# Splitting the branch weights and branch B's result once, ahead of the products that use them

## The chip, the cores and the metric

The kernel runs on one core of a Trainium2 chip. The metric is the device time of one execution in microseconds (us), the median over runs. Five engines work beside each other, each through its own instructions in order: PE (TensorE, matmuls; its weight loads are listed as PEld), DVE (VectorE), ACT (ScalarE), POOL (GpSimd) and SP (SyncE, which here only issues DMA transfers).

## The reference

One layer over 2048 latent tokens and 256 context tokens, width 1024. What matters here:

```
p = layernorm_modulated(x) @ w_in + b_in          # q,k,v, z_A, decays, x_in, B, C, z_B, g_a, g_b
o_a = gated delta rule, 8 heads, both directions, chunks of 64, over q, k, v
y_a = rmsnorm(o_a) * o_norm_w * silu(z_a)
y_b = B * (conv3(C * x_in) + bias) * silu(z_B)
merged = sigmoid(g_a) * (y_a @ w_a) + sigmoid(g_b) * (y_b @ w_b)
out = layernorm(alpha * x + gate * (merged @ w_out)) * ln_g + ln_b
```

All is float32. `w_a` and `w_b` are 1024 x 1024.

## The kernel before

Large products are made in two parts. A float32 operand is split into a high part (a cast to `float32r`) and a low part (the operand less its high part), and a product is three matmuls: high x high, high x low, low x high. `split` (L350) is that: one cast on ACT (L352) and one subtraction (L353) on POOL, or on DVE where the caller asks.

The program has three stages.

1. **Projections** (`projections`, `units`, `strassen`). Tokens are taken in two pairs of 512. Each pair has 40 units (4 each of k, v and q, 16 of branch B, 12 of gates), and a unit is a block of 256 columns of `w_in`, multiplied by a 2x2 Strassen-like scheme of seven products of 12 matmuls. After each product `run_due` (L831) counts one tick and runs what `later` (L827) has put down for that tick. The results go to DRAM tensors: q, k, v, gates, and branch B's `y_b` (`yb_d`), which `evac_z` (L568) writes as plain float32, 256 KB for each 128 x 512 tile.
2. **Window** (`window`). The delta rule walks 36 chunk visits (18 chunks in two directions). The order on PE is written out by hand; the other engines' orders come from a planner. Each visit is a long chain of small DVE steps: decays (L140), the 16 x 16 inverse by 15 rounds of shuffle, multiply and add (L191 to L193), Gram products (L167), state updates (L302, L333). Between the visit's own matmuls PE takes about 24 matmuls of the branch products out of the generator `fillers`. There are eight jobs in it, four of `y_b @ w_b` and then four of `y_a @ w_a`; a job is a block of 512 tokens, with eight products `m` of 24 matmuls. A job's operand is eight tiles `ah`/`al`, filled by `feed` (L1162); a product's weights come from `load_w` (L337).
3. **Tail** (`final`). What is left of the jobs runs while the operands of `w_out` are prepared (`self.tail` is true, and the splits of weights use DVE), then the output projection and the layer norm.

In the window and the tail, `load_w` loads a 512 KB block of raw weights (128 partitions, eight pieces of 512 B each) and splits it: 64 times in all, since each of the two matrices is loaded by four jobs. `feed` loads `y_b` or `y_a` and splits it, 32 times for each:

```
raw = self.wp.tile([P, KT, n], F32, name="wraw", bufs=2)
nc.sync.dma_start(raw, src[:, c0:c0 + n].rearrange("(k p) n -> p k n", p=P))
return self.split_w(raw, n)
```

The load for product `m + 1` is written behind the third group of matmuls of product `m`.

Of the kernel before, what the change touches and what calls it, by code (L numbers as in the profile page):

```python
# [7 lines left out]
F32 = mybir.dt.float32  # L8
FR = mybir.dt.float32r
# [6 lines left out]
P = 128  # L16
D = 1024
KT = 8
H = 8
# [18 lines left out]
class Kern:  # L38
# [297 lines left out]

    def load_w(self, src, c0, n=P):  # L337

        nc = self.nc
        raw = self.wp.tile([P, KT, n], F32, name="wraw", bufs=2)  # L340
        nc.sync.dma_start(raw, src[:, c0:c0 + n].rearrange("(k p) n -> p k n", p=P))
        return self.split_w(raw, n)

    def split_w(self, raw, n=P):
        wh = self.wp.tile([P, KT, n], FR, name="wh")
        wl = self.wp.tile([P, KT, n], FR, name="wl")
        self.split(wh, wl, raw, self.tail and self.nc.vector)
        return wh, wl

# [15 lines left out]
    def build(self, I, out):  # L365
# [15 lines left out]
        self.v_d = [dt(f"vd{i}", [n // P, P, H, P]) for i, n in enumerate(lens)]  # L381
        self.yb_d = [dt(f"ybd{i}", [H, P, 512]) for i in range(4)]
        self.za_d = [dt(f"zad{i}", [4, P, H, P]) for i in range(4)]
# [47 lines left out]
    def projections(self, es, eb, cp):  # L431
# [15 lines left out]
        for c in ORDER:  # L447
            bp = br if c in LATE else bl
            for k in range(4):
                self.B[c, k] = bp.tile([P, 512], FR, name=f"bh{c}{k}"), bp.tile([P, 512], FR, name=f"bl{c}{k}")  # L450
        self.eh = ExitStack()
        self.hc = self.pool(self.eh, "hc", side="right").tile([P, KT, 256], F32, name="hc")
# [34 lines left out]
        with self.tc.manual_schedule(engines={mybir.EngineType.PE}):  # L487
            for _ in steps:
                pass

    def tokens_of(self, t):
# [5 lines left out]
    def units(self, pair):  # L497
# [26 lines left out]
        for kind, base in (("k", 8), ("v", 16), ("q", 0)):  # L524
            for h in range(0, H, 2):
                def evac(i, j, src, kind=kind, ct=base + h, h=h):
                    self.qkv_out(src, ct + i, kind, h + i, tts(j), 512)
                add((base + h) * P, evac)
                if pair == 0 and kind == "v":
                    out[-1]["ctx"] = lambda i, ps, h=h: self.qkv_out(ps, 16 + h + i, "v", h + i, 4, 256)  # L530
            if kind == "v" and pair == 0:
                out[-1]["after"] = self.eh.close
            if kind == "k":
                out[-1]["after"] = lambda: self.later(4, root)
# [4 lines left out]
        def branch(m):  # L539
# [28 lines left out]
            def evac_z(i, j, src):  # L568
                zs = c11() if (i, j) == (0, 0) else src
                nc.scalar.activation(out=zs, in_=src, func=AF.Silu, bias=col(3, i))  # L570
                nc.vector.tensor_tensor(out=zs, in0=zs, in1=t[i, j], op=ALU.mult)
                nc.sync.dma_start(self.yb_d[tts(j)][m + i], zs)

# [97 lines left out]
    def renew(self):  # L671

        nc = self.nc
        tiles = {}

        def load(c):
            for k in range(4):
                tiles[c, k] = self.bt.tile([P, 512], F32, name="bt")
                nc.sync.dma_start(tiles[c, k], self.t_d[k]["1732564".index(c)])

        for c in ORDER[:2]:
            load(c)
        for i, c in enumerate(ORDER):
            for k in range(4):
                self.split(*self.B[c, k], tiles.pop((c, k)), nc.vector if k % 2 else None)
            if i + 2 < 7:
                load(ORDER[i + 2])
            yield

    def gate_rows(self, pool):  # L690
# [462 lines left out]
    def window(self, es, settle):  # L1153
        tc, nc, I = self.tc, self.nc, self.I
        fa = es.enter_context(tc.tile_pool(name="fa", bufs=1, side="right", reuse_waits="tile"))
        fe = es.enter_context(tc.tile_pool(name="fe", bufs=2, side="right", reuse_waits="tile"))
        w_b, w_a = I["w_b"][0], I["w_a"][0]

        self.gk = self.pool(self.ek, "gk", side="right")
        cur = {k: (fa.tile([P, 512], FR, name=f"ah{k}"), fa.tile([P, 512], FR, name=f"al{k}")) for k in range(KT)}  # L1160

        def feed(src, k, eng=None):  # L1162
            if self.yx and k in (3, 4):
                yr = self.yx.tile([P, 512], F32, name=f"yx{k}")
            else:
                yr = fe.tile([P, 512], F32, name="yr", bufs=3)
            nc.sync.dma_start(yr, src[k])
            self.split(*cur[k], yr, eng)
# [23 lines left out]
        ready = lambda j: j[0] == "b" or done.issuperset(GROUPS[j[1]])  # L1192
        operand = lambda j: (self.yb_d if j[0] == "b" else self.ya_d)[j[1]]

        self.job_at, self.tail = 0, False

        for k in range(KT):
            feed(operand(jobs[0]), k, nc.vector if k % 2 else None)
        w0 = self.load_w(w_b, 0)
        while self.pending:  # L1200
# [4 lines left out]
        def fillers():  # L1205
# [3 lines left out]
            for jn, job in enumerate(jobs):  # L1209
# [6 lines left out]
                if not fed:  # L1216
                    for k in range(KT):
                        feed(operand(job), k, nc.vector if self.tail and k % 2 else None)
                W = w_b if job[0] == "b" else w_a
                w = w or self.load_w(W, 0)  # L1220
# [3 lines left out]
                for m in range(8):  # L1224
# [4 lines left out]
                    for k in range(KT):  # L1229
# [6 lines left out]
                        if m == 7 and fed:  # L1236
                            feed(operand(nxt), k, nc.vector if self.tail and k % 2 else None)
                        if k == 2 and m < 7:
                            w = self.load_w(W, (m + 1) * P)
                        if k < KT - 1:  # L1240
# [387 lines left out]
```

## Time and profile before

| | |
|---|---|
| median of 3 runs | 3256.98 us (3252.83 to 3262.17) |
| the profiled execution's own time | 3256.67 us |
| its span (first to last instruction) | 3255.0 us |
| busy share of the span: PE, DVE, POOL, ACT | 91%, 71%, 50%, 48% |
| moved by DMA | 481.75 MB, mean 148 GB/s |
| mean granted TensorE clock | 0.958 |

A busy share is a mean over stages with different limits, so the stages are read one by one: the projections end at about 1818 us of the span, the window at about 2930 us, the last branch product at about 3064 us. A busy PE is not PE at its peak, since matmuls overlap. A line of the code can be that of a helper: L352 and L353 are all splits, told apart by their tiles.

### The profile page before, as it was taken

How to read it: one execution, taken by the hardware profiler on the slowest of the kernel's cores; microseconds unless marked ns; L12 is line 12 of the kernel's file. 1: busy time of each engine (PE TensorE's matmuls, PEld its weight loads, DVE VectorE, ACT ScalarE, POOL GpSimd, SP SyncE). 2: the span in 40 equal slices, each digit the busy share in tenths (PEclk: the TensorE clock that was granted, in tenths of full speed). 3: DMA queues.
4: the chain of work that ended last, by engine and by line, in shares of the span. 5: the costliest groups of instructions: out<-in, count | busy, mean ns of one | idle time of the engine just before them, and what ended most of it. 6: DMA issues, size and time to landing. Idle time of an engine off the chain costs nothing.

```text
span 3255.0 us, 60533 instructions
## 1 busy us (share of the span) xinstructions
PE 2961.8 (91%) x22089; PEld 2438.2 (75%) x22089; DVE 2296.2 (71%) x5815; ACT 1562.2 (48%) x3453; POOL 1622.9 (50%) x1156
## 2 busy tenths in 40 slices
PE   7899999999998899999999888888888888898987
PEld 4677778888886777888888677777777677786766
DVE  7656645555655664555732679999998999978699
ACT  4664633333456645333344355555555666664221
POOL 3444557766666554666666343343343234425464
PEclk9999999999999999999999989989989889999999
DMA  5533322224564432222233655565566667667742
GB/s 211 143 103 89 101 69 88 85 72 148 179 180 141 113 96 78 71 72 65 85 118 91 211 175 177 170 198 173 173 204 217 207 225 239 226 215 247 229 139 101
DMA packets 423047, 481.75 MB, mean 148 GB/s; under 512 B 25428, under 2 KB 324949, under 8 KB 421724
## 3 DMA queue, kind: packets, MB, share of 16 engines
q1 hardware_dynamic: 413646, 470.43, 46.1%
q10 hardware_dynamic: 9102, 7.45, 0.7%
q8 instruction: 173, 2.83, 0.4%
q14 instruction: 126, 1.03, 0.1%
HBM read 341.32 MB, written 136.47 MB: 147 GB/s over the span
## 4 chain that ended last, share of the span: by engine, by line
PE 46%; DVE 29%; issue 7%; ACT 5%; DMA 5%; POOL 4%; SPq 0%; DVEq 0%; POOLq 0%; ACTq 0%
PE pd L747 12%; PE pd L748 12%; PE pd L749 12%; DVE rb L192 4%; DVE gcb L140 4%; DVE R L193 3%; POOL al L353 2%; DVE rb L191 2%; DMA gcb<-gcd 2%; POOL s L733 1%; DVE t L992 1%; ACT n L177 1%; DVE N L167 1%; PE pst L320 1%; DVE QK L167 1%
## 5 line engine op out<-in xcount | busy, mean ns | idle before, releaser
L747 PE MATMUL pd<-bh,ah 128*128 128x512 f32 x2240 | 888.8, 397 | 10.0 <-ACT u L767 5.8
L749 PE MATMUL pd<-bh,al 128*128 128x512 f32 x2240 | 876.1, 391 | 0.0
L748 PE MATMUL pd<-bl,ah 128*128 128x512 f32 x2240 | 875.5, 391 | 0.0
L353 POOL TENSOR_TENSOR al<-s,ah 128x512 fp32r<-128x512 f32 x348 | 478.7, 1378 | 413.7 <-ACT ah L352 397.3
L353 POOL TENSOR_TENSOR al<-raw,ah 128x512 fp32r<-128x512 f32 x260 | 365.2, 1407 | 338.9 <-ACT ah L352 305.8
L747 PEld LDWEIGHTS pd<-bh,ah 128*128 128x128 f32 x2240 | 423.2, 189 | 97.8 <-issue 6.6
L749 PEld LDWEIGHTS pd<-bh,al 128*128 128x128 f32 x2240 | 422.6, 189 | 90.3 <-POOL al L353 0.2
L748 PEld LDWEIGHTS pd<-bl,ah 128*128 128x128 f32 x2240 | 423.4, 189 | 84.8
L352 ACT CAST ah<-s 128x512 fp32r<-128x512 f32 x352 | 215.5, 619 | 332.9 <-PE pd L748 305.8
L352 ACT CAST ah<-raw 128x512 fp32r<-128x512 f32 x264 | 162.6, 617 | 242.4 <-PE pd L748 205.9
L733 DVE TENSOR_TENSOR s<-s,raw 128x512 f32<-128x512 f32 x80 | 119.7, 1497 | 221.1 <-POOL s L733 221.1
L1235 PE MATMUL pf<-ah,wl 128*128 128x512 f32 x512 | 221.5, 433 | 5.3 <-DVE wl L353 3.1
L1231 PE MATMUL pf<-ah,wh 128*128 128x512 f32 x512 | 214.8, 420 | 11.2 <-DVE R L193 5.4
L1233 PE MATMUL pf<-al,wh 128*128 128x512 f32 x512 | 215.3, 421 | 7.5 <-POOL al L353 3.7
L192 DVE TENSOR_TENSOR rb<-rb,n 128x8 f32<-128x8 f32 (+6 forms) x540 | 202.7, 377 | 5.0
L353 POOL TENSOR_TENSOR wl<-wraw,wh 128x1024 fp32r<-128x1024 f32 x48 | 116.9, 2437 | 176.7 <-ACT wh L352 59.4
L140 DVE SCALAR_TENSOR_TENSOR gcb<-gcb,gc,mask 128x128 f32<-128x128 f32 x288 | 179.8, 629 | 8.6 <-ACT qd L137 7.7
L138 POOL TENSOR_TENSOR qd<-qd,qT 128x1024 f32<-128x1024 f32 x32 | 76.4, 2387 | 198.6 <-ACT qd L137 186.3
L193 DVE TENSOR_TENSOR R<-R,rb 128x8 f32<-128x8 f32 (+6 forms) x540 | 157.0, 292 | 5.4
L320 PE MATMUL pst<-S,qd 128*128 128x128 f32 x512 | 112.4, 305 | 39.5 <-ACT ot L1269 23.5
L1009 ACT ACTIVATE t<-t 128x512 f32<-128x512 f32 (+1 forms) x112 | 67.3, 601 | 141.8 <-DVE t L994 141.8
L772 DVE TENSOR_TENSOR u<-pd,u 128x512 f32<-128x512 f32 x80 | 55.0, 688 | 106.6 <-PE pd L749 95.7
(348 smaller groups left out, 6237.2 us busy)
## 6 DMA issues: line engine op xcount, KB each, us to landing
raw<-in_w_in SPq DMA_DIRECT2D x160, 512.0 KB, 3.9
kT<-kTd SPq DMA_DIRECT2D x36, 512.0 KB, 5.2
gcb<-gcd SPq DMA_DIRECT2D x36, 512.0 KB, 4.4
kt<-kd SPq DMA_DIRECT2D x36, 512.0 KB, 3.7
vh<-vd SPq DMA_DIRECT2D x36, 512.0 KB, 3.6
wraw<-in_w_b SPq DMA_DIRECT2D x32, 512.0 KB, 5.0
qT<-qTd SPq DMA_DIRECT2D x32, 512.0 KB, 3.6
wraw<-in_w_a SPq DMA_DIRECT2D x32, 512.0 KB, 4.5
```

What stands on the lines that cost most here:

```text
L140: nc.vector.scalar_tensor_tensor(out=gcb[:, h, :], in0=gcb[:, h, :], scalar=gcT[:, h:h + 1], in1=self.mask[d], op0=ALU.subtract, op1=ALU.min)
L192: nc.vector.tensor_tensor(out=rbv, in0=rbv, in1=bc(n16[:, :, i:i + 1], w), op=ALU.mult)
L193: nc.vector.tensor_tensor(out=R[:, :, c0:c1], in0=R[:, :, c0:c1], in1=rbv, op=ALU.add)
L352: self.nc.scalar.copy(out=hi, in_=src)
L353: (eng or self.nc.gpsimd).tensor_tensor(out=lo, in0=src, in1=hi.bitcast(F32), op=ALU.subtract)
L733: eng.tensor_tensor(out=o, in0=a, in1=b, op=op)
L747: mm(ps, hi[:, k, :], bh, start=(first and k == 0), stop=False, skip_group_check=not first)
L748: mm(ps, hi[:, k, :], bl, start=False, stop=False, skip_group_check=not first)
L749: mm(ps, lo[:, k, :], bh, start=False, stop=(last and k == 3), skip_group_check=not first)
L1231: mm(ps, wh[:, k, :], ah, start=(k == 0), stop=False)
L1233: mm(ps, wh[:, k, :], al, start=False, stop=False)
L1235: mm(ps, wl[:, k, :], ah, start=False, stop=(k == KT - 1))
```

## The change

The parts of the weights are made once and kept in DRAM (`w_d`). `parts_of_w`, called where the context tokens' buffer `hc` is given up (behind the last v unit of the first pair), puts down sixteen jobs, one each 14 ticks, for eight blocks of `w_b` and eight of `w_a`: load 512 KB raw, cast on ACT, subtract on DVE, store the two parts of 512 KB. Each block is stored as 128 rows of 4 KB. `load_w` then only loads the two parts, into three buffers of each instead of two of raw, two of high and two of low part.

`evac_z` splits branch B's result as it is made (cast on ACT, subtraction on DVE) and stores both parts, 256 KB each. `feed` of a B job loads both parts straight into `ah` and `al`; a feed of an A job is as before. The on-chip space that the program keeps for descriptors of software-made DMAs is cut to 512 B for each partition.

```
-    def load_w(self, src, c0, n=P):
-        raw = self.wp.tile([P, KT, n], F32, name="wraw", bufs=2)
-        nc.sync.dma_start(raw, src[:, c0:c0 + n].rearrange("(k p) n -> p k n", p=P))
-        return self.split_w(raw, n)
-    def split_w(self, raw, n=P):
-        wh = self.wp.tile([P, KT, n], FR, name="wh")
-        wl = self.wp.tile([P, KT, n], FR, name="wl")
-        self.split(wh, wl, raw, self.tail and self.nc.vector)
-        return wh, wl
+    def load_w(self, w, m):
+        parts = [self.wp.tile([P, KT, P], FR, name=n, bufs=3) for n in ("wh", "wl")]
+        for t, src in zip(parts, self.w_d[w][m]):
+            self.nc.sync.dma_start(t.bitcast(F32), src)
+        return parts
...
-                out[-1]["after"] = self.eh.close
+                out[-1]["after"] = self.parts_of_w
...
-                nc.sync.dma_start(self.yb_d[tts(j)][m + i], zs)
+                yh = ph["ev"].tile([P, 512], F32, name="yh")
+                self.split(yh, zs.bitcast(FR), zs, nc.vector)
+                for dst, part in zip(self.yb_d[tts(j)], (yh.bitcast(F32), zs)):
+                    nc.sync.dma_start(dst[m + i], part)
...
+    def parts_of_w(self):
+        nc = self.nc
+        self.eh.close()
+        pool = self.pool(self.ehw, "pw", side="right")
+        def part(w, m):
+            raw = pool.tile([P, KT, P], F32, name="raw")
+            nc.sync.dma_start(raw, self.I[w][0][:, m * P:m * P + P].rearrange("(k p) n -> p k n", p=P))
+            hi, lo = (pool.tile([P, KT, P], FR, name=n) for n in ("hi", "lo"))
+            self.split(hi, lo, raw, nc.vector)
+            for dst, src in zip(self.w_d[w][m], (hi, lo)):
+                nc.sync.dma_start(dst, src.bitcast(F32))
+        for i in range(16):
+            self.later(4 + 14 * i, lambda i=i: part(("w_b", "w_a")[i // 8], i % 8))
...
-        def feed(src, k, eng=None):
+        def feed(job, k, eng=None):
+            if job[0] == "b":
+                for t, src in zip(cur[k], self.yb_d[job[1]]):
+                    nc.sync.dma_start(t.bitcast(F32), src[k])
+                return
+            src = self.ya_d[job[1]]
...
-                            w = self.load_w(W, (m + 1) * P)
+                            w = self.load_w(W, m + 1)
...
-    nc = _bacc.Bacc("TRN2", target_bir_lowering=False, num_devices=1)
+    nc = _bacc.Bacc("TRN2", target_bir_lowering=False, num_devices=1, dynamic_dma_scratch_size=512)
```

## Rows read from the trace of the kernel before

**Rows 1.** Busy time of each engine in four stretches; columns in its first line.

```profile
core 0: us, PE busy (x) PEld busy (x) DVE busy (x) ACT busy (x) POOL busy (x), PEclk, DMA share, GB/s
300.00:930.00 630.00, 625.56 (x2825) 506.73 (x2826) 362.77 (x551) 260.23 (x526) 390.23 (x289) 1.00 0.37 110
930.00:1818.00 888.00, 859.32 (x3836) 699.96 (x3836) 462.02 (x628) 398.84 (x839) 527.77 (x394) 0.99 0.34 98
1830.00:2930.00 1100.00, 931.66 (x13082) 813.86 (x13083) 986.14 (x3860) 641.96 (x1504) 409.45 (x265) 0.91 0.61 201
2930.00:3070.00 140.00, 123.62 (x527) 95.87 (x526) 112.67 (x132) 55.14 (x104) 60.03 (x38) 0.95 0.78 241
```

**Rows 2.** Chain of work that ended last, 1830 to 2930 us, shares by line.

```profile
by line: DVE rb L192 11.3%; DVE gcb L140 11.1%; DVE R L193 8.0%; DVE rb L191 6.0%; DMA gcb<-gcd 4.9%; issue 4.4%; ACT n L177 3.3%; DVE N L167 3.3%; PE pst L320 2.8%; DVE QK L167 2.7%; DVE S L333 2.3%; PE pst L321 2.2%; DVE vh L302 2.1%; PE 
```

**Rows 3.** Groups, 1830 to 2930 us: busy us, mean ns | idle before.

```profile
L140 DVE SCALAR_TENSOR_TENSOR gcb<-gcb,gc,mask 128x128 f32<-128x128 f32 x283 | 177.3, 630 | 7.7 <-ACT qd L137 7.7
...
L353 POOL TENSOR_TENSOR wl<-wraw,wh 128x1024 fp32r<-128x1024 f32 x45 | 109.8, 2441 | 163.0 <-ACT wh L352 59.4 <-PE pf L1235 48.1 <-ACT qd L137 23.1
...
L333 DVE SCALAR_TENSOR_TENSOR S<-S,d,pst 128x128 f32<-128x128 f32 x256 | 84.7, 341 | 0.0
...
L353 POOL TENSOR_TENSOR al<-yr,ah 128x512 fp32r<-128x512 f32 x40 | 51.1, 1294 | 32.0 <-ACT ah L352 31.2 <-PE pinv L278 0.8
...
L352 ACT CAST wh<-wraw 128x1024 fp32r<-128x1024 f32 x45 | 46.8, 1040 | 10.6 <-PE pf L1233 2.7 <-DMA wraw<-in_w_a 2.3 <-POOL wl L353 2.0
```

**Rows 4.** Single lines, whole execution: shortest, median and longest duration in ns.

```profile
L140 DVE SCALAR_TENSOR_TENSOR gcb<-gcb,gc,mask x288: 309/343/2569, 1826.8 to 2871.5; 128x128 f32<-128x128 f32 x144
...
L192 DVE TENSOR_TENSOR rb<-rb,n x540: 124/227/2459, 1837.4 to 2897.3; 128x8 f32<-128x8 f32 x35, 128x32 f32<-128x32 f32 x35, 128x56 f32<-128x56 f32 x35, 128x80 f32<-128x80 f32 x35
...
L193 DVE TENSOR_TENSOR R<-R,rb x540: 154/227/2421, 1837.6 to 2897.7; 128x8 f32<-128x8 f32 x35, 128x32 f32<-128x32 f32 x35, 128x56 f32<-128x56 f32 x35, 128x80 f32<-128x80 f32 x35
```

**Rows 5.** Groups of the page, whole execution, the same two lines.

```profile
L192 DVE TENSOR_TENSOR rb<-rb,n 128x8 f32<-128x8 f32 (+6 forms) x540 | 202.7, 377 | 5.0
...
L193 DVE TENSOR_TENSOR R<-R,rb 128x8 f32<-128x8 f32 (+6 forms) x540 | 157.0, 292 | 5.4
```

**Rows 6.** Timeline inside one visit: start us, us, engine, line, operation.

```profile
2134.42 2.36 POOL L353 TENSOR_TENSOR wl<-wraw,wh 128x1024 fp32r<-128x1024 f32 x1 [10.83 <-PE pf L1235]
...
2134.91 1.98 DVE L192 TENSOR_TENSOR rb<-rb,n 128x96 f32<-128x96 f32 x1
...
2136.73 2.42 POOL L138 TENSOR_TENSOR qd<-qd,qT 128x1024 f32<-128x1024 f32 x1
...
2136.82 2.48 DVE L140 SCALAR_TENSOR_TENSOR gcb<-gcb,gc,mask 128x128 f32<-128x128 f32 x1
```

**Rows 7.** Busy time in three visits, cut at L198's start; columns of Rows 1.

```profile
2333.28:2364.06 30.78, 25.79 (x373) 22.84 (x373) 28.24 (x109) 16.66 (x36) 11.05 (x8) 0.94 0.47 164
2364.06:2397.60 33.54, 26.56 (x377) 23.46 (x378) 30.31 (x109) 17.59 (x36) 14.84 (x11) 0.92 0.55 182
2397.60:2430.72 33.12, 27.41 (x368) 24.47 (x368) 31.12 (x110) 20.60 (x43) 17.66 (x14) 0.86 0.69 238
```

**Rows 8.** DMA queue, 1830 to 2930 us: packets, MB, share of 16 engines.

```profile
q1 hardware_dynamic: 140948, 219.11, 60.5%
```

**Rows 9.** DMA issues, whole execution: count, KB each, us to landing.

```profile
kt<-kd SPq DMA_DIRECT2D x36, 512.0 KB, 3.7
...
wraw<-in_w_b SPq DMA_DIRECT2D x32, 512.0 KB, 5.0
```

**Rows 10.** Chain of work that ended last, 2930 to 3070 us, shares by line.

```profile
by line: issue 14.1%; DMA mt<-mbd 9.7%; DVE gt L1187 7.7%; DVE ow L1452 7.2%; DVE ol L353 6.9%; DVE wl L353 6.7%; DMA raw<-mgd 6.5%; DMA yr<-yad 4.4%; DMA ow<-in_w_out 4.2%; DVE al L353 4.1%; DVE ow L1461 3.6%; DMA mgd<-gt 2.9%; DVE gt L118
```

**Rows 11.** Line L353 on DVE: shortest, median and longest duration in ns.

```profile
L353 DVE TENSOR_TENSOR wl<-wraw,wh x16: 1211/1350/2300, 2943.8 to 3057.7; 128x1024 fp32r<-128x1024 f32 x16
```

**Rows 12.** Tile gw, split in the projections: durations in ns; idle time before it.

```profile
L352 ACT CAST gwh<-gw x16: 602/619/624, 430.9 to 622.2; 128x512 fp32r<-128x512 f32 x16
...
  ACT gwh L352: 0.5, 1
```

More of the change, by code (lines that the diff above doesn't have):

```diff
@@ L334, in st_u @@
                                                in1=pu[:, h - 4 * g, :], op0=ALU.mult, op1=ALU.add)
-    def load_w(self, src, c0, n=P):
-        nc = self.nc
-        raw = self.wp.tile([P, KT, n], F32, name="wraw", bufs=2)
-        nc.sync.dma_start(raw, src[:, c0:c0 + n].rearrange("(k p) n -> p k n", p=P))
-        return self.split_w(raw, n)
-    def split_w(self, raw, n=P):
-        wh = self.wp.tile([P, KT, n], FR, name="wh")
-        wl = self.wp.tile([P, KT, n], FR, name="wl")
-        self.split(wh, wl, raw, self.tail and self.nc.vector)
-        return wh, wl
+    def load_w(self, w, m):
[3 more added lines that the diff above has]
+        return parts
     def split(self, hi, lo, src, eng=None):
@@ L381, in build @@
         self.v_d = [dt(f"vd{i}", [n // P, P, H, P]) for i, n in enumerate(lens)]
-        self.yb_d = [dt(f"ybd{i}", [H, P, 512]) for i in range(4)]
+        self.yb_d = [[dt(f"yb{p}d{i}", [H, P, 512]) for p in "hl"] for i in range(4)]
+        self.w_d = {w: [[dt(f"{w}{p}d{m}", [P, KT, P]) for p in "hl"] for m in range(8)] for w in ("w_b", "w_a")}
         self.za_d = [dt(f"zad{i}", [4, P, H, P]) for i in range(4)]
@@ L450, in projections @@
                 self.B[c, k] = bp.tile([P, 512], FR, name=f"bh{c}{k}"), bp.tile([P, 512], FR, name=f"bl{c}{k}")
-        self.eh = ExitStack()
+        self.eh, self.ehw = ExitStack(), ExitStack()
         self.hc = self.pool(self.eh, "hc", side="right").tile([P, KT, 256], F32, name="hc")
@@ L489, in projections @@
                 pass
+        self.ehw.close()
     def tokens_of(self, t):
@@ L571, in evac_z @@
                 nc.vector.tensor_tensor(out=zs, in0=zs, in1=t[i, j], op=ALU.mult)
-                nc.sync.dma_start(self.yb_d[tts(j)][m + i], zs)
+                yh = ph["ev"].tile([P, 512], FR, name="yh")
+                self.split(yh, zs.bitcast(FR), zs, nc.vector)
+                for dst, part in zip(self.yb_d[tts(j)], (yh.bitcast(F32), zs)):
+                    nc.sync.dma_start(dst[m + i], part)
             for seg, evac in ((0, evac_x), (2, evac_c), (1, evac_b), (3, evac_z)):
@@ L1156, in window @@
         fe = es.enter_context(tc.tile_pool(name="fe", bufs=2, side="right", reuse_waits="tile"))
-        w_b, w_a = I["w_b"][0], I["w_a"][0]
         self.gk = self.pool(self.ek, "gk", side="right")
         cur = {k: (fa.tile([P, 512], FR, name=f"ah{k}"), fa.tile([P, 512], FR, name=f"al{k}")) for k in range(KT)}
-        def feed(src, k, eng=None):
+        def feed(job, k, eng=None):
[4 more added lines that the diff above has]
+            src = self.ya_d[job[1]]
             if self.yx and k in (3, 4):
@@ L1192, in window @@
         ready = lambda j: j[0] == "b" or done.issuperset(GROUPS[j[1]])
-        operand = lambda j: (self.yb_d if j[0] == "b" else self.ya_d)[j[1]]
         self.job_at, self.tail = 0, False
         for k in range(KT):
-            feed(operand(jobs[0]), k, nc.vector if k % 2 else None)
-        w0 = self.load_w(w_b, 0)
+            feed(jobs[0], k)
+        w0 = self.load_w("w_b", 0)
         while self.pending:
@@ L1217, in fillers @@
                     for k in range(KT):
-                        feed(operand(job), k, nc.vector if self.tail and k % 2 else None)
-                W = w_b if job[0] == "b" else w_a
+                        feed(job, k, nc.vector if self.tail and k % 2 else None)
+                W = "w_b" if job[0] == "b" else "w_a"
                 w = w or self.load_w(W, 0)
@@ L1236, in fillers @@
                         if m == 7 and fed:
-                            feed(operand(nxt), k, nc.vector if self.tail and k % 2 else None)
+                            feed(nxt, k, nc.vector if self.tail and k % 2 else None)
                         if k == 2 and m < 7:
-                            w = self.load_w(W, (m + 1) * P)
+                            w = self.load_w(W, m + 1)
                         if k < KT - 1:
```

## The prediction

> **What bounds the kernel now.** I read first the busy time by stage [rows 1]. In the projections PE is the bound: 625.6 of 630 us, then 859.3 of 888 us. In the window it is not: of 1100 us PE is busy 931.7, DVE 986.1, POOL 409.5, ACT 642.0. So I read the window's chain of waits next [rows 2]: L192, L140 and L193 alone, small DVE steps, are 11.3 + 11.1 + 8.0 = 30.4% of it, 334 us. The window goes at the pace of a string of DVE instructions, with PE filling in.
>
> Then the durations of these steps [rows 3 to 5]. L140 takes 343 ns as a median, and 630 as a mean in the window, with a longest of 2569. L192 and L193 have a median of 227 and means of 377 and 292. L333, which takes one input from PSUM, has a mean of 341: it is not lengthened. The timeline of one visit shows by what the others are [rows 6]. POOL's `wl` subtraction runs from 2134.42 to 2136.78, and an L192 that starts beside it takes 1.98 us and ends with it (2136.89). POOL's next one runs to 2139.15, and an L140 takes 2.48 us and ends with that (2139.30). A DVE instruction with both inputs in SBUF thus waits out a POOL instruction that reads SBUF. Long POOL work costs DVE time, though POOL is busy only 37% of the window.
>
> How much: L140 283 x (630 - 343) = 81 us; L192 540 x (377 - 227) = 81 us; L193 540 x (292 - 227) = 35 us; 197 us together. Over POOL's 409.5 us that is 0.48 us for each us of POOL. (The medians mix shapes, and nearly all of L192 and L193 lies in the window, so this is an estimate.)
>
> **Taken away from the window.** All 45 `wl` subtractions, 109.8 us of POOL [rows 3], and the subtractions of the three B feeds that lie inside it, 24 of the 40 `al<-yr`, at 1.294 us, 31.1 us: 140.9 us of POOL. At 0.48 that is 68 us of DVE waiting. How much reaches the end?
>
> - A comparison inside the trace answers directly [rows 7]. Visits without a feed take 30.78 us (this one and its two neighbours before it) with 11.05 us of POOL. The two visits in which a job's eight `yr` are split take 33.54 and 33.12 us, with 14.84 and 17.66 us of POOL. So 5.1 us more span for 10.4 us more POOL: 0.49 for each us. 140.9 x 0.49 = 69 us.
> - Lower end: only the share of these instructions that lies on the chain counts. That is 334 us of 177.3 + 202.7 + 157.0 = 537 us busy, 0.62, and 68 x 0.62 = 42 us.
> - Upper end: every removed instruction held DVE as the one in rows 6 did. That L192 works on 96 elements, fewer than the 128 of L140 with its 343 ns, so it lost at least 1.64 us to a POOL instruction of 2.36: 0.69, and 98 us.
>
> I take 69, since two ways agree on it. ACT also loses 45 x 1.040 + 24 x 0.619 = 62 us of casts; it is busy 58% of the window, and I count nothing more for that, since the feed visits lost ACT work too.
>
> The page "SBUF — State Buffer" of the Trainium skill, section "Who interferes with whom", says that the two engines share a read port as an exclusive lock, and that the loser is fully blocked for the other's whole instruction. Taken so far that each removed us of POOL had blocked DVE, the sum would be 141 us in place of 69; the rows agree with the lock, and not with its being hit every time.
>
> **Added to the window: transfers.** 48 weight loads grow by 0.5 MB and 24 feeds by 0.25 MB: 30 MB. At the window's own price, 60.5% of 1100 us for 219.11 MB, 3.04 us of all 16 engines for each MB [rows 8], that is 91 us. The busy share would go from 0.61 to (671 + 91) / 1031 = 0.74. Bounds: nothing, if all of it lands early. Or what is on the chain grows as the share does: `gcb<-gcd` is 4.9%, 54 us, and 54 x 0.13 / 0.61 = 12 us. The parts are loaded a whole product ahead, into three buffers, so that the slot has long been free, and SP no longer waits for POOL there. A block with rows of 4 KB (`kt`) lands in 3.7 us, raw weights in 5.0 [rows 9]. I take 8 us lost. Window: 69 - 8 = 61 us gained. Its head I count at nothing: the first branch product can't start before the projections' last, and what it waits for afterwards changes from splits to loads.
>
> **The tail.** The sixteen `wl` on DVE are 6.7% of its chain of 140 us, 9.4 us [rows 10], which go. Against that 16 x 0.5 = 8 MB are added, 24 us of the engines by the same price, in a stretch whose DMA share is 0.78 [rows 1]: (109 + 24) / 140 = 0.95. Transfers are 9.7 + 6.5 + 4.4 + 4.2 + 2.9 = 27.7% of this chain, 39 us; grown as the share, 39 x 0.17 / 0.78 = 8.5 us lost. So from 9 gained to 9 lost; I take 3 gained, since the added bytes come in the long rows of `kt`'s kind.
>
> The page "DMA: Bandwidth & Descriptors" of the Trainium skill, section "Where 436 GB/s comes from", gives some 358 GB/s as HBM's limit for one core. By it the tail's 241 GB/s and 8 MB more in 140 us, 301 GB/s (an estimate), would still fit, and the loss would be nothing.
>
> **Moved into the projections.** ACT gets 16 x 1.040 + 32 x 0.619 = 36 us. DVE gets 16 x 1.35 us [rows 11] and 32 of half that, 43 us, or up to 74 at the longest duration. SP gets 32 more stores of `y_b`, and 16 loads and 32 stores of parts; queued behind them are the raw blocks of `w_in`, which are loaded one unit ahead. All this lies beside PE's products: in 300 to 930 us, where the sixteen parts fall, DVE is busy 58% and ACT 41% [rows 1]. The nearest row for the new wait (load, cast and subtraction written together, so that ACT could stand still until the load lands) is `gw`, done the same way in the same stage: sixteen casts, and 0.5 us of idle time in all [rows 12]. Cost: from nothing to 10 us (the instructions that fall on PE's few gaps: 33 us of 1518 are not covered by PE); I take 2. The smaller space for software-made descriptors costs nothing: the transfers here are of the queue's hardware kind [rows 8].
>
> **Sum.** 61 + 3 - 2 = 62 us. The profiled execution took 3256.67 us, 0.3 below the median, so 3256.67 - 62 = 3195 us.
>
> **The rivals.**
>
> - *PE's order takes over.* PE is busy 26 of a visit's 30.8 us, in a fixed order, with its own waits. With DVE quicker those waits end last, and only the lower end is won: 42 - 12 in the window, nothing in the tail, 3257 - 30 = 3227 us. For it: PE's 85%. Against it: the feed visits, which show PE following DVE at once.
> - *The full price of the lock.* 98 - 0 + 9 = 107 us, 3150 us. For it: rows 6, where two POOL instructions in a row each held a DVE one. Against it: the mean of 0.48.
> - *The transfers eat it.* If each of 64 weight products waits 1 us longer for its two loads, 64 us are gone: about 3257 us, no change. For it: the share of 0.95 in the tail, and 0.74 in the window. Against it: three buffers, and in the window a load is written five eighths of a product ahead, which at one product a visit [rows 7] is some 19 us.
> - *Slower, through the projections.* The cast of each part stands on ACT until the raw block lands (5.0 us), and DVE's subtraction (2.3 us at the longest) behind it; PE's casts and PSUM evacuations queue behind both. If all of it reached PE, 16 x (5.0 + 1.0 + 2.3) = 133 us would be lost against 62 won: 3328 us. It decides from about 3.9 us a part. For it: PE has no slack there. Against it: `gw`.
> - *Every removed us had held DVE.* POOL's 140.9 us come back whole: 141 - 8 + 3 - 2 = 134 us, 3123 us. For it: rows 6. Against it: the mean of 0.48 [rows 4, 5]. It is the lock of the page on SBUF, hit every time.
>
> **How the numbers follow.** What this kernel's measurement can tell from no change is 0.3%, some 10 us. Chances: my forecast (some 45 to 90 us won) 0.57; PE's order 0.19; the upper price 0.08; every us 0.02; transfers 0.08; slower 0.06. The range reaches from the upper price to a little past PE's order, 3150 to 3238 us; the case of every us, the transfers and the slower case lie outside. Of the transfers' case I count 0.02 as faster and 0.06 as the same, and of PE's order 0.01 as the same: faster 0.87, same 0.07, slower 0.06.
>
> **What would show it.** In the window no `wl` on POOL and only `al` of the A feeds: POOL near 270 us; L140's mean well below 630, near 500; L333's unchanged at 341; a visit without a feed near 29.5 us, and visits with a B feed no longer than the others. The DMA share near 0.7. In the projections PE still at 99% between 300 and 930 us, and casts of the parts with little idle time ahead of them. I am wrong if L140's mean falls and the visits stay at 30.8 us (PE's order), if PE's waits in the window name loads of `wh` or `wl` (transfers), or if the projections end later than 1818 us by more than 10 us.

## The result, and the profile after

The changed kernel takes 3214.4 us as a median (3213.33 to 3221.24), the kernel before 3255.99 us on the same chip. The ratio is 0.9874, with a 95% interval of 0.9854 to 0.9895: 1.3% faster. The forecast was 3195 us, in a range of 3150 to 3238. The profiled execution went from 3256.67 to 3213.67 us, 43 us less.

The same stages as in [rows 1], cut where they end now (projections to 1842, delta rule visits to 2837, tail to 3019); columns in the first line:

```profile
core 0: us, PE busy (x) PEld busy (x) DVE busy (x) ACT busy (x) POOL busy (x), PEclk, DMA share, GB/s
300.00:930.00 630.00, 612.12 (x2738) 494.09 (x2737) 384.33 (x559) 272.24 (x541) 382.76 (x280) 0.99 0.49 149
930.00:1842.00 912.00, 881.68 (x3933) 717.57 (x3931) 486.34 (x670) 413.74 (x868) 538.55 (x403) 0.99 0.37 107
1886.00:2836.00 950.00, 840.86 (x12569) 736.26 (x12568) 854.28 (x3676) 561.95 (x1366) 259.53 (x193) 0.95 0.72 248
2837.00:3019.00 182.00, 148.09 (x900) 116.69 (x898) 96.79 (x161) 50.42 (x128) 52.85 (x36) 0.92 0.79 261
```

To compare like with like I cut the span at events that both kernels have. The projections end with their last matmul (`pd`). The visits run from the first to the last of the 36 `r32t<-r` transposes (L198), one in each visit; between the two lies the head. The tail runs from the last transpose to the last branch product (`pf`), and the rest is the output projection. The line of L198 in the kernel before and in the changed one (shortest, median, longest ns, then first and last start):

```profile
L198 DVE STREAM_TRANSPOSE r32t<-r x36: 428/445/448, 1863.9 to 2900.8; 128x256 f32<-128x256 f32 x36
```

```profile
L198 DVE STREAM_TRANSPOSE r32t<-r x36: 427/442/446, 1886.0 to 2836.9; 128x256 f32<-128x256 f32 x36
```

Worked out in this way, in us, with the forecast beside it (the window's 61 stand under the visits):

| | before | after | won | forecast |
|---|---|---|---|---|
| projections' end | 1818.9 | 1842.0 | -23.1 | -2 |
| head | 45.0 | 44.0 | +1.0 | 0 |
| visits | 1037.0 | 950.9 | +86.1 | +61 |
| tail | 163.4 | 182.2 | -18.8 | +3 |
| rest | 190.7 | 192.8 | -2.1 | 0 |
| sum | | | 43.1 | 62 |

The total hides three misses. The visits gave 25 us more than forecast, and the projections and the tail took 43 us that the forecast did not see.

**Visits.** The groups of the changed kernel between 1886 and 2836 us (busy us, mean ns | idle before), to be set beside [rows 3]:

```profile
L140 DVE SCALAR_TENSOR_TENSOR gcb<-gcb,gc,mask 128x128 f32<-128x128 f32 x272 | 123.0, 455 | 3.6 <-ACT qd L137 2.7 <-ACT d L134 0.9
L333 DVE SCALAR_TENSOR_TENSOR S<-S,d,pst 128x128 f32<-128x128 f32 x256 | 85.3, 337 | 0.1
...
L347 POOL TENSOR_TENSOR al<-yr,ah 128x512 fp32r<-128x512 f32 x16 | 20.7, 1303 | 14.5 <-ACT ah L346 12.5 <-PE pf L1251 0.9 <-PE gram L1417 0.9
```

L140 fell from 630 to 455 ns, and L333, with its PSUM input, stayed at 337. Over the whole execution L192's mean fell from 377 [rows 5] to 316 ns, and L193's did not move (292, then 293):

```profile
L192 DVE TENSOR_TENSOR rb<-rb,n 128x8 f32<-128x8 f32 (+6 forms) x540 | 170.2, 316 | 4.8
L193 DVE TENSOR_TENSOR R<-R,rb 128x8 f32<-128x8 f32 (+6 forms) x540 | 157.4, 293 | 6.0
```

The visits of the kernel before, cut as those of the changed one; DVE and POOL are busy 938 and 391 us there, and 854 and 260 us now:

```profile
1864.00:2901.00 1037.00, 877.46 (x12566) 767.95 (x12567) 938.13 (x3667) 613.42 (x1430) 391.05 (x257) 0.91 0.61 202
```

On POOL no `wl` is left, and of the `al` those of the A feeds. Three visits without a feed take 27.1 us in the mean, where [rows 7] show 30.78:

```profile
2250.00:2277.50 27.50, 27.34 (x397) 24.63 (x397) 25.95 (x112) 16.40 (x35) 11.47 (x9) 1.00 0.63 207
2277.50:2303.60 26.10, 22.31 (x355) 19.57 (x354) 22.97 (x108) 14.91 (x33) 5.72 (x5) 0.93 0.67 229
2303.60:2331.40 27.80, 27.63 (x401) 25.00 (x401) 26.03 (x111) 16.57 (x35) 11.60 (x9) 1.00 0.59 201
```

**Projections.** 300 to 930 us shows the loss: 2738 matmuls instead of 2825 [rows 1], and 49% DMA share instead of 37%. The line of tile `hi`, the cast of the parts in the changed kernel, and what ACT waited for ahead of it:

```profile
L346 ACT CAST hi<-raw x16: 1031/1048/1056, 324.9 to 482.6; 128x1024 fp32r<-128x1024 f32 x16
...
  ACT hi L346: 29.7, 10
  DMA raw<-in_w_a: 15.5, 6
  DMA raw<-in_w_b: 7.8, 4
```

All sixteen run within 158 us, one each 10.5 us, and ACT stood 23.3 us for raw blocks that had not landed. (The line above those two is DVE's, which waits for the cast.) `gw`, the row that the forecast went by, had 0.5 us [rows 12]. The changed kernel's waits between 300 and 500 us (us in total, times, longest) show who stood behind ACT:

```profile
PEld pt L1033 <- ACT t L1025: 14.1, 9, 3.4
PE pt L1033 <- ACT t L1025: 10.5, 8, 2.9
```

In the kernel before the same two lines have less than half of that in these 200 us:

```profile
PEld pt L1017 <- ACT t L1009: 6.2, 7, 1.1
PE pt L1017 <- ACT t L1009: 3.3, 7, 0.7
```

These are PE's transposes of the v and k results, which need ACT's activation. They are written among PE's products, so the products behind them wait too.

**Tail.** PE's waits of the changed kernel between 2837 and 3019 us name the weights:

```profile
PE pf L1249 <- DMA wh<-w_ahd: 18.7, 5, 12.8
PE pf L1249 <- DVE gt L1205: 7.3, 3, 6.1
PE pf L1253 <- DMA wl<-w_ald: 2.7, 6, 0.8
```

In the kernel before, between 2901 and 3064 us, PE has no such wait for a load; its longest single wait there is

```profile
PE pf L1231 <- DVE gt L1186: 3.3, 1, 3.3
```

### The profile page after: what moved, and what is told of

The parts are those of the page before. It is cut to its first block, busy times and chain, and to the rows that moved or that the text cites. A ratio compares the mean times of both kernels' runs of the same rounds, so it can differ in the third digit from the quotient of the medians.

```text
span 3211.9 us, 60563 instructions
## 1 busy us (share of the span) xinstructions
PE 2935.4 (91%) x22089; PEld 2411.4 (75%) x22089; DVE 2222.2 (69%) x5843; ACT 1512.2 (47%) x3405; POOL 1467.2 (46%) x1080
## 4 chain that ended last, share of the span: by engine, by line
PE 47%; DVE 26%; issue 7%; DMA 6%; ACT 6%; POOL 4%; SPq 1%; DVEq 0%; ACTq 0%; POOLq 0%
PE pd L763 12%; PE pd L764 12%; PE pd L765 12%; DVE R L193 3%; DVE rb L192 3%; POOL al L347 2%; DVE gcb L140 2%; DVE rb L191 2%; DVE t L1008 1%; DMA gcb<-gcd 1%; POOL s L749 1%; PE pf L1253 1%; ACT n L177 1%; PE pf L1249 1%; DVE t L1010 1%
## 5 line engine op out<-in xcount | busy, mean ns | idle before, releaser
L347 POOL TENSOR_TENSOR al<-raw,ah 128x512 fp32r<-128x512 f32 x260 | 372.0, 1435 | 321.7 <-ACT ah L346 296.0
L749 DVE TENSOR_TENSOR s<-s,raw 128x512 f32<-128x512 f32 x80 | 107.1, 1338 | 220.5 <-POOL s L749 216.3
L1249 PE MATMUL pf<-ah,wh 128*128 128x512 f32 x512 | 213.0, 417 | 43.1 <-DMA wh<-w_ahd 20.9
L192 DVE TENSOR_TENSOR rb<-rb,n 128x8 f32<-128x8 f32 (+6 forms) x540 | 170.2, 316 | 4.8
L193 DVE TENSOR_TENSOR R<-R,rb 128x8 f32<-128x8 f32 (+6 forms) x540 | 157.4, 293 | 6.0
L1249 PEld LDWEIGHTS pf<-ah,wh 128*128 128x128 f32 x512 | 101.5, 198 | 65.8 <-issue 32.6
L118 POOL TENSOR_TENSOR kt<-kt,kd 128x1024 f32<-128x1024 f32 x36 | 70.2, 1950 | 154.7 <-DMA kt<-kd 108.9
L140 DVE SCALAR_TENSOR_TENSOR gcb<-gcb,gc,mask 128x128 f32<-128x128 f32 x288 | 127.6, 449 | 4.8 <-ACT qd L137 2.7
L1253 PEld LDWEIGHTS pf<-ah,wl 128*128 128x128 f32 x512 | 101.2, 198 | 29.8 <-DMA wl<-w_ald 9.1
```

What stands on the lines that cost most here:

```text
L140: nc.vector.scalar_tensor_tensor(out=gcb[:, h, :], in0=gcb[:, h, :], scalar=gcT[:, h:h + 1], in1=self.mask[d], op0=ALU.subtract, op1=ALU.min)
L192: nc.vector.tensor_tensor(out=rbv, in0=rbv, in1=bc(n16[:, :, i:i + 1], w), op=ALU.mult)
L193: nc.vector.tensor_tensor(out=R[:, :, c0:c1], in0=R[:, :, c0:c1], in1=rbv, op=ALU.add)
L347: (eng or self.nc.gpsimd).tensor_tensor(out=lo, in0=src, in1=hi.bitcast(F32), op=ALU.subtract)
L749: eng.tensor_tensor(out=o, in0=a, in1=b, op=op)
L1249: mm(ps, wh[:, k, :], ah, start=(k == 0), stop=False)
```

## The experiments

Stages of every run, cut as above, in us; the last columns are L140's mean (ns) and the time with its ratio to the kernel before on the same chip (95% interval). The edits are to the changed kernel unless the text says otherwise.

| run | proj. end | head | visits | tail | L140 | median us | ratio |
|---|---|---|---|---|---|---|---|
| before | 1818.9 | 45.0 | 1037.0 | 163.4 | 629 | 3255.99 | 1 |
| after | 1842.0 | 44.0 | 950.9 | 182.2 | 449 | 3214.4 | 0.9874 (0.9854 to 0.9895) |
| e1_pool_back | 1841.5 | 49.7 | 1015.9 | 178.6 | 534 | 3281.54 | 1.0061 (1.0036 to 1.0087) |
| e2_pool_memset | 1843.3 | 43.9 | 949.8 | 181.6 | 464 | 3212.6 | 0.9846 (0.9823 to 0.987) |
| e3_act_back | 1845.2 | 44.9 | 954.5 | 187.4 | 453 | 3221.25 | 0.987 (0.9853 to 0.9888) |
| e4_spaced | 1827.1 | 42.4 | 951.7 | 182.6 | 450 | 3194.17 | 0.9788 (0.9767 to 0.981) |
| e5_prefetch | 1843.5 | 42.6 | 939.5 | 179.9 | 443 | 3201.49 | 0.9811 (0.9789 to 0.9833) |
| e6_tail_raw | 1840.1 | 43.1 | 954.7 | 161.1 | 450 | 3193.85 | 0.9792 (0.9772 to 0.9813) |
| e7_w_only | 1840.7 | 36.7 | 955.9 | 181.8 | 466 | 3211.24 | 0.9845 (0.9824 to 0.9867) |
| e8_yb_only | 1821.7 | 55.7 | 1019.3 | 163.4 | 619 | 3258.77 | 0.9994 (0.9981 to 1.0007) |
| e9_best_w | 1820.8 | 36.5 | 951.1 | 162.2 | 486 | 3162.24 | 0.9698 (0.9683 to 0.9714) |
| e10_best_all | 1827.8 | 42.8 | 945.2 | 161.7 | 435 | 3169.34 | 0.9718 (0.9703 to 0.9733) |
| e11_head | 1845.1 | 51.5 | 950.6 | 185.7 | 453 | 3224.77 | 0.9885 (0.9867 to 0.9903) |

### What gave the visits their 86 us (e1 to e3)

Three kernels put back one part of the removed work in the window, as work whose result `dz` nobody uses. e1 puts the subtraction back on POOL, e2 the same POOL time as memsets behind a small copy, which hardly read on-chip memory, and e3 the cast on ACT. In `load_w`, behind the loads, with `hi` and `lo` the loaded parts (the lines marked e1, e2 and e3 are three separate edits):

```
+        if not self.tail:
+            dz = self.wp.tile([P, KT, P], F32, name="dz", bufs=1)
+            self.nc.gpsimd.tensor_tensor(out=dz, in0=hi, in1=lo, op=ALU.subtract)   # e1
+            self.nc.gpsimd.tensor_copy(out=dz[:, 0, 0:8], in_=hi[:, 0, 0:8])        # e2
+            for _ in range(2):                                                      # e2
+                self.nc.gpsimd.memset(dz, 0.0)                                      # e2
+            self.nc.scalar.copy(out=dz, in_=hi)                                     # e3, dz of type FR
```

> The changed kernel, with a POOL subtraction of the two parts of each weight block (128x1024, result never used) put back into the window, behind the load. Theory A (the window's gain is DVE no longer waiting out POOL instructions that read SBUF): some 45 instructions of 2.4 us come back, 110 of the 141 us removed, so the stretch from the first to the last L198 (957 us in the changed kernel, 1043 before) grows by 110/141 of 85, some 55 to 75 us, L140's mean goes back towards 600 ns, and the time to about 3280 us. Theory B (the gain is ACT's casts, SP's waits or the direct loads): the stretch grows by under 15 us, the time stays near 3215 to 3230 us.

> The changed kernel, with two memsets of 128x1024 on POOL behind each weight load in the window (tied to the load by a copy of eight columns), which write SBUF and do not read it. Theory A (DVE waits only for POOL instructions that read SBUF): L140's mean stays near 449 ns and the stretch of the visits grows by under 15 us. Theory C (any POOL time costs, because POOL's own queue delays what the visit needs from it): the stretch grows for each us of POOL as in the run with the subtraction, by 0.5 us or so.

> The changed kernel, with a cast of 128x1024 on ACT behind each weight load in the window (result never used), as many as were taken away. Theory A (POOL is what counted): the stretch of the visits grows by under 12 us. Theory B (ACT's relief was a main part of the 85 us): it grows by 25 us or more, time near 3240 us.

e1's visits, then e2's, as windows with the columns above:

```profile
1891.00:2907.00 1016.00, 868.03 (x12583) 755.62 (x12583) 928.22 (x3676) 563.85 (x1369) 354.01 (x234) 0.92 0.68 233
```

```profile
1887.00:2837.00 950.00, 840.19 (x12572) 735.49 (x12572) 855.50 (x3677) 563.26 (x1369) 347.45 (x316) 0.95 0.73 249
```

POOL is busy 354 and 347 us, some 90 us more than in the changed kernel in both. With subtractions DVE's busy time rises by 74 us (854.28 to 928.22) for the same instructions, and the visits by 65 us; with memsets DVE's rises by 1.2 us and the visits by none. e1's timeline shows one such pair, as in [rows 6]:

```profile
2241.25 2.38 POOL L345 TENSOR_TENSOR dz<-wh,wl 128x1024 f32<-128x1024 f32 x1 [2.23 <-DMA wl<-w_bld]
2241.33 2.42 DVE L192 TENSOR_TENSOR rb<-rb,n 128x104 f32<-128x104 f32 x1
```

So it is POOL's reading that costs, not POOL's time nor its place in a queue. (e1's expectation gives the visits as 957 and 1043 us; cut as here they are 950.9 and 1037.0. L140's mean went back to 534 ns, not to 600.) With e3 the visits are 3.6 us longer. That is no more than in e6 (954.7 us), whose edit concerns the tail alone, so ACT's casts are not shown to cost anything. The page "SBUF — State Buffer" of the Trainium skill, section "Who interferes with whom", says that a DVE instruction with two inputs there contends with a GpSimd instruction that reads it, and not with one that only writes it; e1 and e2 agree, with 65 us against -1.

### One half of the change at a time (e7, e8)

e7 keeps the split weights, and stores branch B's result plain, split at the feed as before. e8 keeps that result's split, and loads and splits the weights as before the change.

```
-                yh = ph["ev"].tile([P, 512], FR, name="yh")                         # e7
-                self.split(yh, zs.bitcast(FR), zs, nc.vector)
-                for dst, part in zip(self.yb_d[tts(j)], (yh.bitcast(F32), zs)):
-                    nc.sync.dma_start(dst[m + i], part)
+                nc.sync.dma_start(self.yb_d[tts(j)][0][m + i], zs)
...
-                out[-1]["after"] = self.parts_of_w                                  # e8, load_w as before
+                out[-1]["after"] = self.eh.close
```

> Half of the change: the weights' parts are made in the projections, branch B's result is stored plain and split in the feeds as before. If each removed us of POOL counts alike, the visits' stretch (951 us in the changed kernel, 1037 before) comes to about 970, since 31 of the 141 us of POOL come back; the projections still end about 1838 to 1842 us if the weights' parts are what held them; time about 3228 us. If the feeds at the job boundaries are the larger part, the stretch is above 985 us.

> The other half: branch B's result is split in the projections, the weights are loaded raw and split in the window as before. By POOL time the visits' stretch is about 1018 us (31 of 141 us removed); the projections end by 1824 us if the weights' parts held them; the tail is at 163 us as before if the weight loads' bytes or order are what lengthened it; time about 3240 us. If branch B's split costs the projections, they end above 1828 us.

(As these lines show, `yh` is a tile of type FR, the `float32r` of a high part, in the changed kernel.)

The weights alone are worth the whole change: ratios of 0.9845 and 0.9874, with intervals that overlap. Branch B's split alone is worth nothing (0.9994): its visits are 17.7 us shorter, its head is 10.7 longer, and the projections take 2.8 us. The expectations had e7's visits at 970 us or above and e8's time at 3240; the visits came to 956 us, and e8's long head was not foreseen.

The visits of e7, then of e8:

```profile
1877.00:2833.00 956.00, 847.09 (x12582) 742.08 (x12581) 868.99 (x3680) 574.01 (x1393) 290.95 (x217) 0.94 0.71 241
1877.00:2897.00 1020.00, 866.25 (x12567) 757.09 (x12568) 928.75 (x3669) 598.64 (x1407) 358.29 (x233) 0.92 0.64 210
```

Against the kernel before, e7's POOL is busy 100 us less and its visits are 81 us shorter: 0.81 for each us. For e8 it is 33 us and 17.7: 0.54. But the two do not add up: 81 and 18 make 99, and both together, the changed kernel, won 86. Put on top of the weights (e7 against the changed kernel), branch B's split takes 31 us more off POOL and makes the visits only 5.0 us shorter, 0.16 for each us, while the head is 7.3 us longer. So what a us of POOL is worth depends on what else has gone, and no one rate holds.

### What the projections lost (e4)

e4 ties each part's load to PE's progress: a one-column copy from the last product's PSUM tile into the raw buffer, so that the load waits for that product. It adds sixteen small ACT copies.

```
             raw = pool.tile([P, KT, P], F32, name="raw")
+            nc.scalar.copy(out=raw[:, 0, 0:1], in_=self.last[:, 0:1])
             nc.sync.dma_start(raw, self.I[w][0][:, m * P:m * P + P].rearrange("(k p) n -> p k n", p=P))
...
                 product(u, c, ps, c not in "23", True)
+                self.last = ps
                 self.run_due()
```

> The changed kernel, with the load of each block in the projections made to wait for the product of its tick (one ACT copy of one column from that product's PSUM into the raw tile ahead of the load), so that the sixteen parts come 14 ticks apart and not as soon as their buffer is free. Theory P (the 23 us lost in the projections come from sixteen loads, casts and subtractions bunched into 318 to 486 us, where PE's transposes wait for ACT): the last product of the projections ends near 1826 us and not at 1842, the time falls by 12 to 18 us, to about 3199 us. Theory Q (the added work costs PE the same wherever it is): no change, 3214 us.

e4's casts of the parts:

```profile
L346 ACT CAST hi<-raw x16: 1040/1054/1058, 344.1 to 960.5; 128x1024 fp32r<-128x1024 f32 x16
```

They now run over 616 us, one each 41, and the projections end 14.9 us earlier. Windows of the changed kernel, then of e4, between 300 and 500 us:

```profile
300.00:400.00 100.00, 89.80 (x410) 71.74 (x408) 69.53 (x110) 54.33 (x135) 46.60 (x34) 0.98 0.68 207
400.00:500.00 100.00, 92.77 (x414) 70.39 (x415) 56.90 (x77) 50.84 (x127) 46.94 (x33) 0.97 0.64 200
```

```profile
300.00:400.00 100.00, 94.79 (x444) 76.11 (x442) 65.15 (x116) 55.09 (x145) 49.88 (x36) 1.00 0.47 134
400.00:500.00 100.00, 98.74 (x448) 75.46 (x449) 51.71 (x70) 44.65 (x116) 58.42 (x41) 1.00 0.33 99
```

The same work, paced, gives PE its 11 us of busy time back in these 200 us, and the full granted clock. e4 moves the loads, the casts, the subtractions and the stores together, so it shows that the bunching cost these 15 us; that ACT's stand is the link rests on the wait lines above. Of the 8.2 us that e4 still loses to the kernel before, branch B's split is the largest part: e9, which has paced parts and no such split, ends its projections 1.9 us after the kernel before, and e10, with it, 8.9 us. (Alone, in e8, the split costs 2.8.)

### What the tail lost (e5, e6)

Two causes were open. In the order of SP's queue, a job's first weights are issued only when its products begin, and the longest wait, 12.8 us, is there. The bytes are the other: two parts of 512 KB in place of one raw block. e5 issues the next job's first block one product ahead; e6 loads raw weights in the tail and splits them on DVE, as before the change.

```
                             w = self.load_w(W, m + 1)
+                        elif k == 2 and nxt:                                        # e5
+                            w = self.load_w("w_b" if nxt[0] == "b" else "w_a", 0)
...
-                w = None
...
+        if self.tail:                                                               # e6, in load_w
+            raw = self.wp.tile([P, KT, P], F32, name="wraw", bufs=2)
+            self.nc.sync.dma_start(raw, self.I[w][0][:, m * P:m * P + P].rearrange("(k p) n -> p k n", p=P))
+            parts = [self.wp.tile([P, KT, P], FR, name=n, bufs=3) for n in ("wh", "wl")]
+            self.split(*parts, raw, self.tail and self.nc.vector)
+            return parts
```

> The changed kernel, with the first weight block of each job loaded inside the last product of the job before, as the other blocks are. Theory O (the tail's 19 us come from the order in SP's queue: loads of parts stand behind feeds, gate loads and stores that wait; the longest wait, 12.8 us ahead of the last job's first matmul, is one such): the tail (last state matmul's visit to the last branch product, 182 us) shrinks by about 12 us to some 170, the time to about 3202 us. Theory D (the tail is held by the doubled bytes of the weight loads): the wait only moves, the tail stays at 178 to 184 us.

> The changed kernel, but in the tail (the last 16 products) the weights are loaded raw and split on ACT and DVE as before the change. Theory D (the doubled bytes hold the tail): the tail goes from 182 back to some 165 us, time about 3198 us. Theory O (order of SP's queue alone): the tail stays above 176 us, since the loads stand at the same places of the queue, and DVE gets its 25 us of subtractions back.

With e5 the 12.8 us wait is gone, and the tail is 2.3 us shorter, no more; the longest is now 3.0 us, but PE still waits 10.8 us for `wh` in the tail:

```profile
PE pf L1249 <- DMA wh<-w_ahd: 10.8, 6, 3.0
```

(e5's time fell all the same, since its visits, with job boundaries of their own, are 11.4 us shorter.) With e6 the tail is 21.1 us shorter, though DVE and ACT have their splits back. The tails as windows, of the kernel before, the changed one and e6:

```profile
2901.00:3064.00 163.00, 145.14 (x900) 115.65 (x899) 124.17 (x181) 68.45 (x148) 63.22 (x39) 0.96 0.74 227
```

```profile
2838.00:2999.00 161.00, 143.83 (x902) 117.76 (x901) 119.79 (x181) 66.49 (x146) 59.13 (x37) 0.96 0.76 241
```

The changed kernel's row is the last of the first fence. Share times length is the DMA engines' time: 121 us before, 144 changed, 122 in e6. The tail follows it: 163, 182 and 161 us, at nearly the same share. e7 and e8 say the same: 181.8 us with the weights' parts, 163.4 with raw weights. So the doubled weights cost the tail its time; whether by their bytes or by their doubled number of loads, e6 does not tell apart.

### Putting it together (e9, e10)

e10 is e4, e5 and e6 together; e9 is the same without the split of branch B's result, as in e7.

> The weights' half alone (branch B's result stored plain and split in the feeds, as before the change), with three repairs together: parts spaced by tick, each job's first block loaded in the job before, raw weights split on ACT and DVE in the tail. If the single runs add up: projections end about 1826 us (15 less than in the run of the weights' half), head 37, visits 945, tail 160, rest 191 us: 3159 us, 0.968 of the kernel before. If the repairs overlap (the spaced parts or the early loads collide with something else): above 3180 us.

> The whole change with the same three repairs. If they add up: projections 1827, head 43, visits 940, tail 159, rest 192 us: 3161 us. Theory Y (branch B's split is worth nothing, since the head of the window gives back what the visits win): within 8 us of the run with the weights' half. Rival: it is worth its 31 us of POOL, and this run is 12 us or more quicker than that one.

e9 takes 3162.24 us, 3.0% less than the kernel before and, by the two ratios, 1.8% less than the changed one, and e10 is 7.1 us slower. e9 came within 3 us of the sum of its single runs; e10 is 8 us short of its own, mostly because its visits are 5.7 us shorter than the changed kernel's where e5's were 11.4. The split of branch B's result costs more than it brings: 7.0 us of projections and 6.3 of head, against 5.9 of visits.

### The head (e11)

In the changed kernel the first branch product comes 13.6 us after the projections' end, before the change 0.3. SP has sixteen feed loads to issue ahead of the first weights, and stands twice among them:

```profile
SPq L1179 <- DMA zad<-c: 8.7, 1, 8.7
SPq L1179 <- DMA zad<-u: 6.1, 1, 6.1
```

e11 moves these sixteen loads to ACT's queue.

```
-        def feed(job, k, eng=None):
+        def feed(job, k, eng=None, q=nc.sync):
...
-            feed(jobs[0], k)
+            feed(jobs[0], k, q=nc.scalar)
```

> The changed kernel, with the sixteen loads of the first job's parts issued from ACT's queue and not from SP's. Theory H (the head of the window, from the projections' last product to the first L198, 44 us, holds a wait of SP's queue: kT, gcb and the first weight parts stand behind feed loads that wait): the first branch product starts within 6 us of the projections' end (13.6 before), and the head shrinks to about 36 us, the time to about 3207 us. Rival: the loads wait for bytes and not for the queue, head 42 to 46 us.

The first product now comes 0.8 us after the projections' end, and the head is 7.5 us longer, 51.5 us. ACT's own last gate activations stood behind the loads that it issued (the timeline of e11, with the idle time before in brackets):

```profile
1856.90 0.69 ACT L602 ACTIVATE c<-pd,biasT 128x512 f32<-128x512 f32 x1 [18.50 <-DMA al<-ybld]
```

Neither expectation held. Since ACT stood, e11 does not show what an early first product alone is worth; the kernel before had one at 0.3 us, with a head of 45.0 us. That plain feeds together with the weights' parts shorten the head (36.7 us in e7, 36.5 in e9) is measured; which wait sets it was not settled.

## Why the prediction was right, and where it was not

- **The mechanism of the window was right.** DVE's wait for POOL's reads is what went, as e1 and e2 show; L333 kept its duration, and the DMA share came to 0.72 against "near 0.7". The visits with a B feed became no longer than the others (25.1 and 27.0 us for the third job), except the first feed's, right behind the head: 35.7 and 21.6 us, before 36.9 and 29.8. One term was not there: L140's and L192's means account for DVE's gain (180 ns x 288 = 52 us, 61 ns x 540 = 33 us), and L193, to which the forecast gave 35 us of waiting, lost nothing.
- **The window's size was 25 us short; the step is the rate of 0.49.** In the visits POOL's busy time fell by 131.5 us (391.05 to 259.53), near the 140.9 of the forecast. DVE's fell by 84 us (938.13 to 854.28), where the forecast had 68 by 0.48, and the visits fell by 86: as much as DVE's loss. The 0.49 came from two feed visits against a base of 30.78 us, and that base was high. The same trace has twelve visits without a feed around two feeds (first and third row: six visits each; second and fourth: the two visits of a feed):

```profile
1939.25:2115.71 176.46, 148.28 (x2185) 132.14 (x2186) 162.52 (x645) 95.85 (x197) 65.74 (x47) 0.93 0.51 172
2115.71:2183.82 68.11, 55.15 (x760) 49.31 (x759) 61.86 (x224) 38.91 (x79) 34.50 (x27) 0.90 0.59 193
2183.82:2364.09 180.27, 155.15 (x2249) 137.97 (x2250) 164.40 (x651) 98.53 (x202) 64.36 (x46) 0.95 0.53 174
2364.09:2430.74 66.65, 53.93 (x744) 47.90 (x743) 61.45 (x219) 38.18 (x79) 32.52 (x25) 0.89 0.62 210
```

  The twelve take 29.7 us each with 10.8 us of POOL, and the four feed visits have 15.8 us more span for 23.7 us more POOL: 0.67, and 94 us for 140.9. The runs give 0.69 (e1), 0.81 (e7), 0.54 (e8) and 0.16 (branch B's split on top of the weights), so even a better base gives no fixed price. The forecast's upper price, 0.69, from a long pair [rows 6], was nearer. Why the rates differ, by the length of an instruction (2.4 us for weights, 1.3 for feeds), its place in the chain or what else waits, was not tested.
- **The 8 us for the window's transfers were sought at the wrong place.** The chain of the changed kernel has `gcb<-gcd` at 4.4% of 950 us, 42 us, where [rows 2] give 54: no loss. But four loads of weights stand on it, 21.8 us together, where the kernel before has one, of 6.7 us. The longest is

```profile
2191.89 7.32 DMA wh<-w_bhd
```

  "Loaded a whole product ahead" holds for a job's later blocks; its first is issued only when the job begins. e5, which issues it earlier, has one such load left on the chain (4.0 us) and visits that are 11.4 us shorter; in e9 and e10, which hold the same edit, they are 5 to 6 us shorter than in e7 and the changed kernel. PE's own waits in the visits name `wh` or `wl` for 4.5 us, so this sign of being wrong showed in small.
- **The projections failed at the step "nearest row".** `gw` was taken as the price of the parts' wait, 0 to 10 us, and the loss was 23; the forecast's own sign, an end more than 10 us late, came true. The parts are not spread over 14 ticks each on the chip: nothing ties them to PE's progress, so they ran as fast as one raw buffer allowed. ACT stood for landings, and PE's transposes stood behind ACT. This is the rival "slower, through the projections" in kind, at a sixth of its 133 us. e4 shows that the bunching is 15 of the 23 us.
- **The tail failed at the step that let the share rise.** The 24 us of added DMA time were right (23 measured). The forecast let them fill the tail's free share, up to 0.95, and charged only the chain's transfers, 8.5 us at most. The share stayed near 0.8, and the tail grew by 18.8 us. (The 23 were right partly by chance: the stretch moved 47.5 MB where it had moved 37.0, more than the 8 added, at less time for each MB.) The page "DMA: Bandwidth & Descriptors" of the Trainium skill, section "Where 436 GB/s comes from", puts the limit at some 358 GB/s; the changed tail moved 261 GB/s in the mean and was held all the same, so its limit gave no warning here.
- **The head at nothing was right in the sum** (1 us), by luck: the weights' parts make it 8.3 us shorter (e7 against the kernel before), and feeds that are loaded in two parts 7.3 us longer.
- "PE's order takes over" did not come about: the visits won more than the middle value. "The transfers eat it" came about in the tail alone, where PE's waits name the weights; it took 19 us there and not 64.

That the total came near is luck in part: the window's surplus of 25 us covers a good half of the 43 us by which the projections and the tail missed.

## What to carry to other kernels

Where DVE sets the pace, POOL work that reads on-chip memory cost 0.5 to 0.8 us for each of its us here, and moving it away paid; but the second piece moved was worth only 0.16, so price a piece with the others already gone. A price read from a few visits needs a base of all the like visits in the trace. Work that is moved into a stage bound by PE needs something that ties it to PE's progress, or it comes in one lump and holds the engines that PE waits for. Doubled loads cost at most some 11 us (e5) in the visits, which make a product in 23.5 us at a DMA share of 0.72, and nearly their whole transfer time in the tail, which makes one in 9.4 us at 0.79 (971 and 463 `pf` matmuls, 24 to a product): one change can take parts in one stage and the raw form in the next.

## What the runs showed of the hardware

A POOL memset of 0.95 us held no DVE instruction noticeably: 82 of them in e2's visits left DVE's busy time within 1.2 us of the changed kernel's. And a short stand of PE in the projections can cost more than its own length. In the changed kernel's timeline of PE, with idle time before in brackets, matmuls of one shape take 0.63 us behind the second of two such stands and 0.39 us a little later:

```profile
377.94 0.66 PE L1033 MATMUL pt<-ident,t 128*128 128x128 f32 x4 [2.10 <-ACT t L1025]
...
386.62 0.98 PE L1033 MATMUL pt<-ident,t 128*128 128x128 f32 x4 [1.92 <-ACT jk L1043]
...
388.68 0.63 PE L763 MATMUL pd<-bh,ah 128*128 128x512 f32 x1
...
391.02 0.39 PE L764 MATMUL pd<-bl,ah 128*128 128x512 f32 x1
```

The granted clock is 0.50, the lower of its two levels (1.2 GHz), from 387 to 390 us, and 1.00 again from 391 to 394 us; columns as in the first fence:

```profile
387.00:390.00 3.00, 3.00 (x10) 2.42 (x9) 1.07 (x2) 2.84 (x15) 2.17 (x2) 0.50 1.01 358
```

Behind the first stand, of 2.10 us, one matmul took 0.48 us and the next ones 0.39. Over 300 to 400 and 400 to 500 us, the two stretches that hold such stands, the mean is 0.98 and 0.97, and 1.00 in e4's.
